# Two weight sums of the MLP's late down steps made early and kept in DRAM, and the pairs of their group in another order

## The chip, the cores and the metric

The kernel runs on one core of one Trainium2 chip. The metric is device microseconds of one execution, as the median of several runs. The engines are named as in the profile: PE is TensorE's matmul unit and PEld its weight loads, DVE is VectorE, ACT is ScalarE, POOL is GpSimd, and SP is SyncE, which here only issues DMAs.

## The reference, cut to what matters

One layer of a transformer-like trunk: a gated linear attention mixer, then a squared-ReLU MLP, each behind an RMSNorm and with a residual, and a last RMSNorm. All in float32, 256 tokens (T), model width 2048 (D), hidden width 8192.

```python
h = h + _gla_mixer(_rmsnorm(h, gla_norm[j]), ...)
h = h + _sq_relu_mlp(_rmsnorm(h, mlp_norm[i]), mlp_w_up[i], mlp_w_down[i])
return _rmsnorm(h, final_norm)

def _sq_relu_mlp(h, w_up, w_down):
    a = jax.nn.relu(h @ w_up)
    return (a * a) @ w_down
```

The change is in the last product, `(a * a) @ w_down`, of which one hidden slice and one group of 512 output columns are concerned.

## The kernel before

**Numbers.** Every float32 operand is split into two fp32r parts, `hi` (a rounded copy, made by a cast on ACT, line 123) and `lo` (the rest, a subtraction on DVE, lines 136, 170 and 1291). A product is then three matmuls: hi x hi, hi x lo, lo x hi. A matmul here is 128 rows by 256 columns (one of the 256s is T or half of a group of 512).

**Up and down steps.** The MLP runs over 8 rounds (`ROUNDS`) of 1024 hidden values. An up step takes two 128-row tiles of `w_up` for 512 hidden values, 24 matmuls; there are 128 of them (`UPS`). A down step takes a *pair* `kp` (0 to 3) of two 128-row tiles of `w_down` for a round `m` and a group `g` of 512 output columns. The program first makes 18 up steps alone (`LEAD`), and then one up step to each down step, until the up steps end; the down steps after that are alone again (`alone`). Rounds go through the groups forwards and backwards in turn, so that round 6 (`ROUNDS - 2`) ends with group 0 and round 7 begins with it.

**Two kinds of down step.** A plain one takes 2x2 blocks of activations times 2x2 blocks of weights as 8 block products, 24 matmuls. A step *by sums* (`by_sums`) does it with 7 block products of Strassen's kind, 21 matmuls, in two parts: three products from the weights as they are (9 matmuls), and four from sums and differences of the four weight blocks (12 matmuls). The sums are made in place in the raw weight tile: one block by an accumulating DMA from POOL (line 1231) and the others by two subtractions on DVE (`weight_sums`, lines 233 and 234), and are then split into hi and lo again (lines 123 and 1291). A step by sums so costs PE three matmuls less, and ACT and DVE more. Round 6's last group had one step by sums (`kp == 1`) and three plain ones; in round 7 three pairs are by sums.

In a lone step by sums the second part is issued late (`pending`): after the next step's first products.

**Sums from DRAM.** In the mixer's output product, four pairs already get their sums from DRAM: `make_sums` loads the pair in an earlier stage where the engines have time, forms the sums (line 252 and `weight_sums`), splits them (lines 255 and 259), and writes hi and lo (512 KB each) to DRAM by two DMAs from POOL (lines 256 and 260). `make_all` hands out the jobs; `MADE_AT` has, for each stage, the places in its sequence of `pump` calls (two to an up step) at which a job's two halves run. `group` reads them back into `pre` (line 330).

**Buffers.** A weight tile goes through a ring of seven raw tiles and a ring of five hi/lo pairs (pool `wpool`). An SP load waits until DVE has made `lo` from the tile that had its place; a cast waits until PE (or a DMA that reads it) is done with the hi tile. The activations of a round are two tiles `act`, tags B (pairs 0 and 1) and C (pairs 2 and 3) in the pool `big`, two buffers each.

**Order.** A scheduler with a timeline of its own orders the instructions of each engine; each engine then takes them strictly in that order, and waits by semaphores. `last_turn` (lines 978 to 987), which runs among the first lone up steps, transposes the last quarter of h (`hh`, `hl`: ACT line 856, DVE line 857) for the last two up steps of the first half-round.

Of the kernel before, what the change touches and what calls it, by code (L numbers as in the profile page):

```python
# [37 lines left out]
KT = D // P  # L38
# [9 lines left out]
G = 1024  # L48
# [21 lines left out]
def tile_gla_mlp(ctx, tc, x, xt, cols, w_vg, w_in, w_gate, w_out, w_up, w_down, final_norm, out):  # L70
# [54 lines left out]
    def slots():  # L125
        return [wpool.tile([P, SLOT], F32R, tag=i, name=i) for i in ("hi", "lo")]
# [105 lines left out]
    def weight_sums(u):  # L232
        nc.vector.tensor_tensor(u[:, 2], u[:, 0], u[:, 2], op=ALU.subtract)  # L233
        return nc.vector.tensor_tensor(u[:, 1::2], u[:, 1::2], u[:, 2:3].to_broadcast([P, 2, T]), op=ALU.subtract)  # L234
# [29 lines left out]
    def make_all():  # L264
        pair = lambda w, c0, g: w[c0 : c0 + 2 * P, g * GT : (g + 1) * GT].rearrange("(i p) c -> p i c", p=P)
        todo = [make_sums((None, g, kp), pair(w_out, 2 * kp * P, g)) for g, kp in MADE_OUT]
        todo += [make_sums((ROUNDS - 1, g, kp), pair(w_down, (ROUNDS - 1) * MR + 2 * kp * P, g)) for g, kp in MADE_DOWN]
        for places in MADE_AT:
            now = [lambda: None] * (KT - 1)
            for at in places:  # L270
                now[at], now[at + 1] = todo.pop(0)
            yield now
# [907 lines left out]
    def settle(*ks):  # L1180

        for k in ks:
            late.pop(k, lambda: None)()

    def down(passes):
# [4 lines left out]
        ahead = pending = None  # L1190
        quick = False
        units = 0
        for n, (m, g) in enumerate(passes):
            fresh = not n or passes[n - 1][1] != g
            if fresh:
# [6 lines left out]
            first = min(kp for kp in range(KP) if by_sums(m, g, kp)) if fresh else None  # L1202

            if fresh:
                quick = first == 0
            for kp in range(KP):
                last = ends and kp == KP - 1
                alone = units + LEAD >= UPS
                by_parts = by_sums(m, g, kp)

                def products(n, these, w, banks=banks, last=last):

                    with then_mm():
                        for k, o, a, c in these:
                            bank = banks[k][1]
                            for x in a[: 2 - n]:
                                for d in range(0, c.stop - c.start, T):
                                    matmul(
                                        bank[:, o + d : o + d + T], x, w[n][:, c.start + d : c.start + d + T],
                                        bank.name not in used, last and n == 1,  # L1220
                                    )
                                    used.add(bank.name)

                raw = raw_tile()[:, : 2 * GT]
                c0 = m * MR + 2 * kp * P
                src = w_down[c0 : c0 + 2 * P, g * GT : (g + 1) * GT].rearrange("(i p) c -> p i c", p=P)
                if by_parts:
                    for i in range(2):
                        last_load[0] = nc.sync.dma_start(out=raw[:, i * GT : (i + 1) * GT], in_=src[:, i])
# [5 lines left out]
                if fresh and quick and kp < 2:  # L1235
                    pass
                elif fresh and kp == 0:
                    banks.update({k: begin(k, g) for k in (B32, BX4)})
                elif fresh and kp == first:
                    settle(P16)  # L1240
                    banks[P16] = begin(P16, g)
                elif fresh and kp > first and P57 not in banks:
# [22 lines left out]
                if fresh and kp == first and not quick and not alone:  # L1265
# [5 lines left out]
                def of_sums(u=raw, products=products, at=at, kp=kp, banks=banks, quick=fresh and quick, g=g, then=ahead_of):  # L1271


                    nonlocal ahead
                    to = slots()

                    if quick and kp < 2:
                        settle((B32, P16)[kp])
                        if kp == 0:
                            banks[P57] = begin(P57, g)  # L1280
                    if then and by_sums(*then, 0):
                        ahead = {k: begin(k, then[1]) for k in (B32, P16)}
                    for a in range(2):
                        copy_hi(*(x.rearrange("p (f s) -> p f s", f=4)[:, a::2] for x in (to[0][:, :G], u)))
                    if quick and kp == 0:
                        settle(P57)
                        banks[BX4] = begin(BX4, g)
                    elif quick and kp == 1:
                        settle(BX4)
                    with tc.issue_after(last_lo[0].ins):  # L1290
                        last_lo[0] = nc.vector.tensor_tensor(to[1][:, :G], u, to[0][:, :G].bitcast(F32), op=ALU.subtract)  # L1291
                    early = (P57, 0, at(S1), block(0)), (P16, T, at(S2), block(2))
                    late = (P57, T, at(S3), block(1)), (BX4, T, at(A22), block(3))
                    products(0, early, to)
                    yield
                    products(0, late, to)
                    products(1, (*early, *late), to)

                if by_parts:
                    if alone:  # L1300

                        pending = of_sums()
                    else:
                        rest = of_sums()
                        next(rest)
                yield
                if by_parts and not alone:
                    next(rest, None)
                units += 1
                if last:  # L1310
                    if n + 1 < len(passes):
                        m1, g1 = passes[n + 1]
                        assert by_sums(m1, g1, 0) == bool(ahead)
                    else:
                        last_banks(0)
                if fresh and kp == first + alone and not quick:
                    settle(B32, BX4)
            if ends:

# [153 lines left out]
```

## Time and profile before

| | |
|---|---|
| median of 3 runs | 1040.6 us (1040.2 to 1040.94) |
| the profiled execution's own time | 1040.84 us |
| its span in the trace | 1039.1 us |
| PE busy | 1030.4 us, 99% |
| DVE, ACT, POOL busy | 903.5, 754.1, 134.4 us |
| DMA moved | 240.04 MB, mean 231 GB/s |

1.74 us of the execution lie around the span. The MLP begins at 371.3 us in the span; its lone up steps last until about 420 us, the last up step ends at 982.5 us, and the last product starts at about 1010 us. PE's busy time is wall time during which some matmul is in flight: its matmuls are pipelined, so each shows longer (276 ns) than the pace at which they follow each other.

### The profile page before, as it was taken

To read this page: it belongs to the slowest core of one execution; us is meant where nothing else is said; L and a number is where in the kernel's file an instruction comes from. 1 tells how busy PE (TensorE), PEld (TensorE's weight loads), DVE (VectorE), ACT (ScalarE), POOL (GpSimd) and SP (SyncE) were. 2 spreads that over 40 slices of the span, in tenths; PEclk is the share of its full clock that TensorE was granted. 3 is DMA by queue.
4 is the path that set the end of the run, shared out by engine and by line. 5 is a ranking of instruction groups with operands and counts; after the bars stand their busy time and mean duration, and the time that the engine had idled before them with its cause. 6 is when DMAs were issued, how large, how long until landed. Compare 5 with 4: busy or idle time off the path is not lost.

```text
span 1039.1 us, 23376 instructions
## 1 busy us (share of the span) xinstructions
PE 1030.4 (99%) x9019; PEld 1029.5 (99%) x9019; DVE 903.5 (87%) x1254; ACT 754.1 (73%) x1130; POOL 134.4 (13%) x180
## 2 busy tenths in 40 slices
PE   9999999999999999999999999999999999999997
PEld 9999999999999999999999999999999999999997
DVE  7769768898698866989989999999999999999887
ACT  7775556677576654688779788778778778778685
POOL 0000110210100001111111111111211111111100
PEclk9999999999999999999999999999999999999999
DMA  9967866758977876678888887887887888887772
GB/s 340 334 192 217 263 187 170 210 163 300 308 245 251 250 249 193 189 216 229 228 239 227 231 238 225 236 242 221 245 232 221 244 225 229 243 231 219 231 246 84
DMA packets 128591, 240.04 MB, mean 231 GB/s; under 512 B 11440, under 2 KB 30000, under 8 KB 128352
## 3 DMA queue, kind: packets, MB, share of 16 engines
q1 hardware_dynamic: 107456, 215.32, 64.2%
q0 software_dynamic: 20304, 21.64, 12.2%
q10 hardware_dynamic: 720, 1.60, 0.4%
q8 instruction: 70, 1.15, 0.4%
q14 instruction: 41, 0.34, 0.1%
HBM read 232.22 MB, written 6.29 MB: 230 GB/s over the span
## 4 chain that ended last, share of the span: by engine, by line
PE 99%; issue 0%; ACT 0%; DVE 0%; POOLq 0%; POOL 0%; DVEq 0%
PE up L1021 34%; PE acc L1021 28%; PE acc L305 16%; PE acc L181 10%; PE acc L224 6%; PE aux L224 2%; PE aux L181 1%; PE aux L843 1%; PE aux L696 1%; PE aux L399 0%; ACT sqf L1360 0%; PE acc L595 0%; DVE hf L1432 0%; POOLq L1469 0%; POOL rf L521 0%
## 5 line engine op out<-in xcount | busy, mean ns | idle before, releaser
L123 ACT CAST hi<-raw 128x1024 fp32r<-128x1024 f32 (+4 forms) x654 | 518.2, 822 | 201.1 <-DVE raw L233 66.4
L136 DVE TENSOR_TENSOR lo<-raw,hi 128x768 fp32r<-128x768 f32 (+4 forms) x228 | 233.1, 1032 | 53.6 <-ACT hi L123 50.8
L1021 PE MATMUL acc<-hi,act 128*128 128x256 f32 x1696 | 247.7, 276 | 0.0
L1021 PE MATMUL up<-hh,hi 128*128 128x256 f32 x1024 | 238.7, 276 | 0.0
L1021 PE MATMUL up<-hl,hi 128*128 128x256 f32 x1024 | 238.7, 276 | 0.0
L1021 PEld LDWEIGHTS acc<-hi,act 128*128 128x128 f32 x1696 | 217.6, 188 | 0.0
L170 DVE TENSOR_TENSOR lo<-raw,hi 128x1024 fp32r<-128x1024 f32 x160 | 194.4, 1218 | 22.5 <-ACT hi L123 21.6
L1021 PEld LDWEIGHTS up<-hh,hi 128*128 128x128 f32 x1024 | 192.3, 188 | 0.0
L1021 PEld LDWEIGHTS up<-hl,hi 128*128 128x128 f32 x1024 | 192.3, 188 | 0.0
L1231 POOL DMA_DIRECT2D raw<-in_w_down x112 | 97.1, 867 | 518.4 <-DMA raw<-in_w_down 206.2
L1291 DVE TENSOR_TENSOR lo<-raw,hi 128x1024 fp32r<-128x1024 f32 x112 | 136.3, 1217 | 1.1 <-ACT hi L123 1.1
L1021 PE MATMUL up<-hh,lo 128*128 128x256 f32 x1024 | 137.0, 276 | 0.0
L1021 PE MATMUL acc<-lo,act 128*128 128x256 f32 x848 | 133.9, 276 | 0.0
L1021 PEld LDWEIGHTS up<-hh,lo 128*128 128x128 f32 x1024 | 125.7, 188 | 0.0
L1021 PEld LDWEIGHTS acc<-lo,act 128*128 128x128 f32 x848 | 113.4, 188 | 0.0
L234 DVE TENSOR_TENSOR raw<-raw 128x512 f32<-128x512 f32 x137 | 94.5, 689 | 3.4
L233 DVE TENSOR_TENSOR raw<-raw 128x256 f32<-128x256 f32 x137 | 57.8, 422 | 13.1 <-DMA raw<-in_w_out 10.1
L181 PE MATMUL acc<-hi,xA 128*128 128x256 f32 (+1 forms) x376 | 55.6, 280 | 0.0
L181 PEld LDWEIGHTS acc<-hi,xA 128*128 128x128 f32 x376 | 49.3, 188 | 0.3 <-ACT hi L123 0.2
L224 PE MATMUL acc<-xA,hi 128*128 128x256 f32 x288 | 49.2, 276 | 0.0
L224 PEld LDWEIGHTS acc<-xA,hi 128*128 128x128 f32 x288 | 43.3, 188 | 0.0
L1148 ACT COPY sums<-acc 128x512 f32<-128x512 f32 x46 | 26.8, 583 | 22.6 <-PE acc L1021 22.5
(226 smaller groups left out, 1442.2 us busy)
## 6 DMA issues: line engine op xcount, KB each, us to landing
raw<-in_w_up SPq DMA_DIRECT2D x128, 512.0 KB, 4.3
raw<-in_w_down SPq DMA_DIRECT2D x224, 256.0 KB, 4.3
raw<-in_w_in SPq DMA_DIRECT2D x69, 512.0 KB, 4.6
raw<-in_w_down POOLq DMA_DIRECT2D x112, 128.0 KB, 5.1
raw<-in_w_out SPq DMA_DIRECT2D x22, 512.0 KB, 7.1
raw<-in_w_down SPq DMA_DIRECT2D x16, 512.0 KB, 5.2
raw<-in_w_vg SPq DMA_DIRECT2D x14, 520.0 KB, 8.6
raw<-in_w_out SPq DMA_DIRECT2D x24, 256.0 KB, 5.9
```

Of the source, the lines that this page charges most:

```text
L123: last_hi[0] = nc.scalar.copy(to, raw)
L136: last_lo[0] = nc.vector.tensor_tensor(lo[:, s], raw[:, s], hi[:, s].bitcast(F32), op=ALU.subtract)
L170: last_lo[0] = nc.vector.tensor_tensor(to[1], dst, to[0].bitcast(F32), op=ALU.subtract)
L181: newest[0] = nc.tensor.matmul(o[:, m], x, w[:, m], start=first and c == 0, stop=last, skip_group_check=True).ins
L224: nc.tensor.matmul(o, u[:, i, s], m, start=kt == 0 and n == 0 and j % 2 == 0, stop=kt == KT - 1 and n == 2, skip_group_check=True,)
L233: nc.vector.tensor_tensor(u[:, 2], u[:, 0], u[:, 2], op=ALU.subtract)
L234: return nc.vector.tensor_tensor(u[:, 1::2], u[:, 1::2], u[:, 2:3].to_broadcast([P, 2, T]), op=ALU.subtract)
L305: newest[0] = nc.tensor.matmul(bank[:, o + d : o + d + T], x, w[:, d : d + T], start=(not filled or bank in sums_banks) and bank.name not ...
L1021: newest[0] = nc.tensor.matmul(o, x, w, start=first, stop=last, skip_group_check=True).ins
L1148: last_end[0] = nc.scalar.copy(to, src).ins
L1231: nc.gpsimd.dma_start(out=raw[:, :T], in_=src[:, 0, T:], accum_op=ALU.add)
L1291: last_lo[0] = nc.vector.tensor_tensor(to[1][:, :G], u, to[0][:, :G].bitcast(F32), op=ALU.subtract)
```

## The change

Two more pairs get their sums from DRAM: pairs 0 and 1 of round 6, group 0, the last group of that round. Before, its pairs 0 (plain) and 1 (by sums, summed on the spot) went beside the last two up steps, and pairs 2 and 3 (both plain) were the first two lone steps. Now the group takes its pairs as 2, 3, 0, 1: pairs 2 (plain) and 3 (by sums, summed on the spot) go beside the last two up steps, and pairs 0 and 1 (by sums, the sums from DRAM) are the first two lone ones. So three of its four steps are by sums now, and two of them have nothing to sum on DVE, and read 1.375 MB instead of 0.5 MB. The sums are made by two more jobs at the places 10 and 16 of the lone up steps. `pre`, the tile into which they are read back, takes a buffer of tag C.

```diff
-    MADE_DOWN = ()
-    MADE_AT = ((2,), (4,), (6, 10))
+    MADE_DOWN = ((ROUNDS - 2, 0, 0), (ROUNDS - 2, 0, 1))
+    MADE_AT = ((2,), (4,), (6, 10), (10, 16))
...
+    def pairs_of(m, g):
+        return (2, 3, 0, 1) if m == ROUNDS - 2 and g == order_of(m)[-1] else range(KP)
+
     def by_sums(m, g, kp):
...
-        return m < ROUNDS - 2 or g != order_of(m)[-1] or kp == 1
+        return m < ROUNDS - 2 or g != order_of(m)[-1] or kp in (3, 0, 1)
...
-            for kp in range(KP):
+            for pos, kp in enumerate(pairs_of(m, g)):
...
-                if by_parts:
+                ready = made.get((m, g, kp))
+                if pos == 0 and any((m, g, k) in made for k in range(KP)):
+                    rooms.extend(big.tile([P, 4 * G + 64], F32R, tag="C", name="pre")[:, : 4 * G].rearrange("p (b i c) -> b p i c", b=2, i=2))
+                if ready is not None:
+                    last_load[0] = nc.sync.dma_start(out=raw[:, T:GT], in_=src[:, 0, T:])
+                    last_load[0] = nc.sync.dma_start(out=raw[:, GT:], in_=src[:, 1])
+                    ready_in = rooms.pop(0)
+                    for i in range(2):
+                        last_load[0] = nc.sync.dma_start(out=ready_in[:, i].bitcast(F32), in_=ready[i])
+                    ready = [ready_in[:, i] for i in range(2)]
+                elif by_parts:
...
-                    with tc.issue_after(last_lo[0].ins):
-                        last_sum[0] = weight_sums(u).ins
+                    if ready is None:
+                        with tc.issue_after(last_lo[0].ins):
+                            last_sum[0] = weight_sums(u).ins
...
     n_raw[0] = 0
+    jobs.extend(next(make))
     steps = up()
```

**PE, where the up steps end.** Names: `hi_`/`lo_` are parts of weights by number, `pre` the sums from DRAM, `act` the activations, `acc` the banks. Before, the first two lone down steps are plain (16 matmuls with hi, 8 with lo each):

```order
L1021 MATMUL acc_13122<-hi_13258,act_12149 128x256 x4
L1021 MATMUL acc_13124<-hi_13258,act_12149 128x256 x4
L1021 MATMUL acc_13122<-hi_13258,act_12149 128x256 x4
L1021 MATMUL acc_13124<-hi_13258,act_12149 128x256 x4
L1021 MATMUL acc_13122<-lo_13259,act_12149 128x256 x2
L1021 MATMUL acc_13124<-lo_13259,act_12149 128x256 x2
L1021 MATMUL acc_13122<-lo_13259,act_12149 128x256 x2
L1021 MATMUL acc_13124<-lo_13259,act_12149 128x256 x2
L1021 MATMUL acc_13122<-hi_13295,act_12149 128x256 x4
```

Now there stand the first parts of both steps (6 with hi and 3 with lo each), and then the first step's 12 matmuls with `pre`; the second step's 12 with `pre` come after the plain step that follows (hi_13340):

```order
L1025 MATMUL acc_13216<-hi_13286,act_11604 128x256 x2
L1025 MATMUL acc_13147<-hi_13286,act_11604 128x256 x4
L1025 MATMUL acc_13216<-lo_13287,act_11604 128x256
L1025 MATMUL acc_13147<-lo_13287,act_11604 128x256 x2
L1025 MATMUL acc_13216<-hi_13311,act_11604 128x256 x2
L1025 MATMUL acc_13147<-hi_13311,act_11604 128x256 x4
L1025 MATMUL acc_13216<-lo_13312,act_11604 128x256
L1025 MATMUL acc_13147<-lo_13312,act_11604 128x256 x2
L1025 MATMUL acc_13252<-pre_13141,act_11604 128x256 x2
```

What moved: the second lone step's weights (hi_13295 before, hi_13311 now) are asked for after 9 matmuls instead of 24. On ACT and DVE the rows stand in the same order there; the two steps' casts and subtractions are 128x768 instead of 128x1024.

**DVE, among the first lone up steps.** `lo_` from `w_up`, `hl` of the last transposed quarter of h; before:

```order
L170 TENSOR_TENSOR lo_5100<-raw_5101,hi_5099 128x1024
L976 TENSOR_SCALAR work_4913<-ident_96,r2_4912 128x128
L170 TENSOR_TENSOR lo_5130<-raw_5131,hi_5129 128x1024
L170 TENSOR_TENSOR lo_5160<-raw_5161,hi_5159 128x1024
L170 TENSOR_TENSOR lo_5193<-raw_5194,hi_5192 128x2x512
L857 SCALAR_TENSOR_TENSOR hl_4046<-aux_5064,colt_81,hh_4045 128x256
L857 SCALAR_TENSOR_TENSOR hl_4046<-aux_5065,colt_81,hh_4045 128x256
L857 SCALAR_TENSOR_TENSOR hl_4046<-aux_5064,colt_81,hh_4045 128x256
```

Now, with the semaphores that each waits for (DMASW6 is counted up by the landing of `made_1282<-lo_5121`, which POOL issues):

```order
L252 TENSOR_TENSOR raw_5115<-raw_5115 128x256 [waits DMAHW1_49]
L976 TENSOR_SCALAR work_4915<-ident_96,r2_4914 128x128 [waits Pool_49]
L233 TENSOR_TENSOR raw_5115<-raw_5115 128x256 [waits DVE_49]
L234 TENSOR_TENSOR raw_5115<-raw_5115 128x2x256 [waits DVE_49]
L259 TENSOR_TENSOR lo_5121<-raw_5115,hi_5120 128x1024 [waits PE_49,Activation_49]
L170 TENSOR_TENSOR lo_5143<-raw_5144,hi_5142 128x1024 [waits DMAHW2_49,PE_49,Activation_49]
L170 TENSOR_TENSOR lo_5173<-raw_5174,hi_5172 128x1024 [waits DMAHW3_49,PE_49,Activation_49]
L857 SCALAR_TENSOR_TENSOR hl_4048<-aux_5066,colt_81,hh_4047 128x256 [waits Activation_49]
L857 SCALAR_TENSOR_TENSOR hl_4048<-aux_5067,colt_81,hh_4047 128x256 [waits Activation_49]
L170 TENSOR_TENSOR lo_5206<-raw_5207,hi_5205 128x2x512 [waits DMAHW4_49,DMASW6_49,DVE_49]
L252 TENSOR_TENSOR raw_5227<-raw_5227 128x256 [waits DMAHW5_49]
L857 SCALAR_TENSOR_TENSOR hl_4048<-aux_5066,colt_81,hh_4047 128x256 [waits Activation_49]
```

What moved: a job's four operations stand ahead, and the third `hl` (aux_5066 the second time) stands behind a `lo` whose buffer the job's second write to DRAM must first have left, and behind the second job's first addition.

**SP, some 60 us before the group.** Loads of weights for the coming steps, and now the four loads of `pre`:

```order
L1244 DMA raw_12501<-in_w_down 128x512 [waits DMAHW1_49]
L1240 DMA pre_13141<-made_1282 128x1024 [waits DMAHW2_49,PE_49]
L1240 DMA pre_13141<-made_1282 128x1024 [waits DMAHW3_49]
L1240 DMA pre_13141<-made_1283 128x1024 [waits DMAHW4_49]
L163 DMA raw_12522<-in_w_up 128x2x512 [waits DMAHW5_49,DVE_49]
L1240 DMA pre_13141<-made_1283 128x1024 [waits DMAHW6_49]
L1244 DMA raw_12571<-in_w_down 128x512 [waits DMAHW7_49,DMASW1_49,DVE_49]
```

What moved: the first of the four waits for PE (the round-5 activations whose buffer `pre` takes), and the two weight loads behind it (raw_12498 and raw_12547 before) stand behind it on SP.

More of the change, by code (lines that the diff above doesn't have):

```diff
@@ L266, in make_all @@
         todo = [make_sums((None, g, kp), pair(w_out, 2 * kp * P, g)) for g, kp in MADE_OUT]
-        todo += [make_sums((ROUNDS - 1, g, kp), pair(w_down, (ROUNDS - 1) * MR + 2 * kp * P, g)) for g, kp in MADE_DOWN]
+        todo += [make_sums((m, g, kp), pair(w_down, m * MR + 2 * kp * P, g)) for m, g, kp in MADE_DOWN]
         for places in MADE_AT:
-            now = [lambda: None] * (KT - 1)
+            now = [lambda: None] * max(KT - 1, places[-1] + 2)
             for at in places:
@@ L1201, in down @@
             ends = n + 1 == len(passes) or passes[n + 1][1] != g
-            first = min(kp for kp in range(KP) if by_sums(m, g, kp)) if fresh else None
+            first = [by_sums(m, g, kp) for kp in pairs_of(m, g)].index(True) if fresh else None
             if fresh:
                 quick = first == 0
-            for kp in range(KP):
-                last = ends and kp == KP - 1
+            for pos, kp in enumerate(pairs_of(m, g)):
+                last = ends and pos == KP - 1
                 alone = units + LEAD >= UPS
@@ L1264, in down @@
                 yield
-                if fresh and kp == first and not quick and not alone:
+                if fresh and pos == first and not quick and not alone:
                     settle(P57)
@@ L1269, in down, with of_sums @@
                 ahead_of = passes[n + 1] if last and n + 1 < len(passes) else None
-                def of_sums(u=raw, products=products, at=at, kp=kp, banks=banks, quick=fresh and quick, g=g, then=ahead_of):
+                def of_sums(u=raw, products=products, at=at, pos=pos, banks=banks, quick=fresh and quick, g=g, then=ahead_of, to=ready):
                     nonlocal ahead
[L1275 to L1279, printed above, removed]
+                    copied = not to
+                    to = to or slots()
+                    if quick and pos < 2:
+                        settle((B32, P16)[pos])
+                        if pos == 0:
                             banks[P57] = begin(P57, g)
-                    if then and by_sums(*then, 0):
+                    if then and by_sums(*then, pairs_of(*then)[0]):
                         ahead = {k: begin(k, then[1]) for k in (B32, P16)}
-                    for a in range(2):
+                    for a in range(2 * copied):
                         copy_hi(*(x.rearrange("p (f s) -> p f s", f=4)[:, a::2] for x in (to[0][:, :G], u)))
-                    if quick and kp == 0:
+                    if quick and pos == 0:
                         settle(P57)
                         banks[BX4] = begin(BX4, g)
-                    elif quick and kp == 1:
+                    elif quick and pos == 1:
                         settle(BX4)
-                    with tc.issue_after(last_lo[0].ins):
-                        last_lo[0] = nc.vector.tensor_tensor(to[1][:, :G], u, to[0][:, :G].bitcast(F32), op=ALU.subtract)
+                    if copied:
+                        with tc.issue_after(last_lo[0].ins):
+                            last_lo[0] = nc.vector.tensor_tensor(to[1][:, :G], u, to[0][:, :G].bitcast(F32), op=ALU.subtract)
                     early = (P57, 0, at(S1), block(0)), (P16, T, at(S2), block(2))
@@ L1312, in down @@
                         m1, g1 = passes[n + 1]
-                        assert by_sums(m1, g1, 0) == bool(ahead)
+                        assert by_sums(m1, g1, pairs_of(m1, g1)[0]) == bool(ahead)
                     else:
                         last_banks(0)
-                if fresh and kp == first + alone and not quick:
+                if fresh and pos == first + alone and not quick:
                     settle(B32, BX4)
```

9 lines of the change are left out of this document (5 added, 4 removed).

## The prediction

> **What bounds the kernel now.** The page was read first: its busy shares and its chain of waits. Then the windows of four stretches, and then the timelines of PE, DVE, ACT and SP at the three places that the change touches.
>
> ```profile
> span 1039.1 us, 23376 instructions
> PE 1030.4 (99%) x9019; PEld 1029.5 (99%) x9019; DVE 903.5 (87%) x1254; ACT 754.1 (73%) x1130; POOL 134.4 (13%) x180
> PE 99%; issue 0%; ACT 0%; DVE 0%; POOLq 0%; POOL 0%; DVEq 0%
> ```
>
> PE is busy for 99% of the span, and the chain that ended last runs through PE alone. So PE's time is its number of matmuls times their pace, plus whatever it is made to wait. In the windows, each engine's busy time stands behind the length of the stretch; the last three columns are PE's granted clock, the DMA share and GB/s.
>
> ```profile
> 260.00:280.00 20.00, 20.00 (x179) 20.00 (x178) 10.74 (x12) 9.05 (x9) 2.83 (x4) 1.00 0.97 348
> 380.00:390.00 10.00, 10.00 (x91) 10.00 (x90) 5.88 (x8) 5.17 (x8) 0.00 (x0) 1.00 0.57 173
> 430.00:530.00 100.00, 100.00 (x884) 100.00 (x884) 91.22 (x117) 75.88 (x113) 16.06 (x19) 1.00 0.79 225
> 910.00:960.00 50.00, 50.00 (x444) 50.00 (x443) 47.78 (x62) 40.38 (x61) 7.80 (x9) 1.00 0.81 227
> ```
>
> From 430 to 530 us the pace is 100.00 us / 884 = 113.1 ns, at a full clock. DVE is the next engine: 91% busy there and 96% from 910 to 960 (47.78 of 50), but 59% in the lone up steps at 380 to 390, where the new jobs stand.
>
> **The matmuls removed.** Two of the group's plain steps become steps by sums, 21 matmuls instead of 24. That is 2 x 3 x 113.1 ns = 0.68 us, all on PE and so all on the path, if PE goes on without a wait. Nothing else can come off PE's time, so this is also the most that the change can gain.
>
> **The first two lone steps.** PE's side of the place, by start and duration:
>
> ```profile
> 983.39 1.98 PE L1021 MATMUL acc<-hi,act 128*128 128x256 f32 x16
> 986.11 1.98 PE L1021 MATMUL acc<-hi,act 128*128 128x256 f32 x16
> 988.83 1.41 PE L1021 MATMUL acc<-hi,act 128*128 128x256 f32 x11
> ```
>
> And what makes the parts, on DVE and on ACT, and the two rows for their shorter forms (the mean ns of one stands behind the bar):
>
> ```profile
> 979.05 1.23 DVE L136 TENSOR_TENSOR lo<-raw,hi 128x1024 fp32r<-128x1024 f32 x1 [0.55 <-ACT hi L123]
> 982.45 1.29 DVE L1111 SCALAR_TENSOR_TENSOR work<-up,work 128x512 f32<-128x512 f32 x2 [2.17 <-PE up L1021]
> 984.84 1.22 DVE L136 TENSOR_TENSOR lo<-raw,hi 128x1024 fp32r<-128x1024 f32 x1
> 987.23 1.22 DVE L136 TENSOR_TENSOR lo<-raw,hi 128x1024 fp32r<-128x1024 f32 x1
> ```
>
> ```profile
> 983.18 0.63 ACT L1122 ACTIVATE work<-work 128x512 f32<-128x512 f32 x1 [4.16 <-DVE work L1111]
> 983.72 1.03 ACT L123 CAST hi<-raw 128x1024 fp32r<-128x1024 f32 x1
> 985.01 1.05 ACT L1133 CAST act<-work 128x1024 fp32r<-128x1024 f32 x1 [0.26 <-DVE work L1126]
> 985.96 1.05 ACT L123 CAST hi<-raw 128x1024 fp32r<-128x1024 f32 x1
> ```
>
> ```profile
> L136 DVE TENSOR_TENSOR lo<-raw,hi 128x768 fp32r<-128x768 f32 x8 | 7.6, 951 | 0.2 <-ACT hi L123 0.2
> L123 ACT CAST hi<-raw 128x768 fp32r<-128x768 f32 x7 | 5.7, 831 | 0.0
> ```
>
> The first lone step's `lo` is made at 979, 4 us early. The second one's cast (983.72) stands on ACT behind a square, which had waited 4.16 us for DVE's work on the last up product; its `lo` (984.84) stands behind the same work on DVE, which had waited 2.17 us for PE. The end of the up product sets these times, and the order of both engines is unchanged there, so a shorter lone step brings neither forward. Before, PE asked for this hi at 986.11. Now it asks for it after 9 matmuls:
>
> - PE starts the first lone step at 983.39 as before (the two steps ahead have 24 + 21 matmuls in either order). 9 x 0.113 gives 984.41.
> - The second step's hi is ready at 983.72 + 0.83 = 984.55: PE waits 0.14 us. Six matmuls later it is 985.23.
> - Its lo is ready at 984.84 + 0.95 = 985.79: PE waits 0.56 us. Three matmuls end at 986.13.
> - 12 with `pre` end at 987.49. The plain step's hi is there at 985.96 + 1.05 = 987.01, and its lo at 987.23 + 1.22 = 988.45, 0.8 us ahead of its use at 989.30. With 24 + 12 more matmuls it is 991.56.
>
> Before, the same point was 988.83 + 24 x 0.113 = 991.54. The new wait of 0.70 us so takes the whole 0.68 us, and the net is +0.02 us. Its bounds: -0.68 if ACT and DVE run these two operations earlier than the walk has them, and +0.3 if the shorter forms take as long as the two rows they replace (1.03 and 1.22 us: waits of 0.34 and 0.63). I take the walk.
>
> Behind it everything stands as before. The act tile that now takes the just-freed buffer is written at 985.01, 1.5 us after PE has left it at about 983.5. `pre` is read 60 us after its loads. The smaller casts and subtractions and the missing accumulating DMA take work off ACT, DVE and POOL that PE doesn't wait for. All this is costed at nothing; if the buffer did come late, its own cast would slip, and the two casts and PE's plain steps behind it.
>
> **The two jobs among the lone up steps.** The two write rows are the landing times of hi and of lo:
>
> ```profile
> 376.27 0.28 DVE L976 TENSOR_SCALAR work<-ident,r 128x128 f32<-128x128 f32 x1
> L857 DVE SCALAR_TENSOR_TENSOR hl<-aux,colt,hh x4: 477/484/485, 384.8 to 387.9; 128x256 fp32r<-128x256 f32 x4
> 389.28 0.28 PE L1021 MATMUL up<-hl,hi 128*128 128x256 f32 x1
> 390.19 0.28 PE L1021 MATMUL up<-hl,hi 128*128 128x256 f32 x1
> ```
>
> ```profile
> L234 DVE TENSOR_TENSOR raw<-raw 128x512 f32<-128x512 f32 x8 | 5.5, 692 | 0.3
> L233 DVE TENSOR_TENSOR raw<-raw 128x256 f32<-128x256 f32 x8 | 3.4, 422 | 0.2
> ```
>
> ```profile
> DMA to landing us min/median/max: 3.1/3.8/7.0
> ```
>
> ```profile
> L260 POOL DMA_DIRECT2D made<-lo x4: 533/541/553, 95.8 to 266.3; - x4
> who waited for it (us, times):
>   DVE lo L170: 0.5, 1
> DMA to landing us min/median/max: 6.5/6.9/7.1
> ```
>
> A job costs DVE two additions, a double subtraction and a split, 0.42 + 0.42 + 0.69 + 1.22 = 2.75 us and ACT one cast; for two jobs that is 5.5 us of DVE, while in the lone steps it is free 4.1 us in every 10. PE's cost is nothing, unless the order makes something late, and one thing is near: the third `hl`, wanted at 390.19. It stands behind a `lo` whose buffer the job's second write must have left. The first job's sums follow the work at 376.27 and end at about 377.9; cast and subtraction bring it to about 380.2; POOL's issue follows some 0.3 us later, at 380.5. With landings of 6.5 to 7.1 us that is 387.0 to 387.6. Then come that `lo` (1.22), the second job's first addition (0.42) and the `hl` (0.48): 389.1 to 389.7. The margin is 0.5 to 1.1 us. The write of hi holds up a cast on ACT in the same way, with the first `hl` behind it: at 3.8 us nothing is late, at 7.0 us the cast starts at about 386.2 and the third `hl` ends some 0.4 us late. So the price is 0 to 0.4 us by the rows, and I take 0; a write that lands later costs PE one for one. The Trainium skill ("DMA: Bandwidth & Descriptors", section "Anatomy of one DMA — SWDGE (gpsimd) path") fits such a DMA with 2.0 us plus its bytes over 436,000 per us, an estimate of 3.2 us for 512 KB; by that the margin would be over 4 us and this price surely none. The four lo writes took 6.5 to 7.1 us here, twice that, and the rows decide.
>
> **The loads of `pre` on SP.**
>
> ```profile
> 907.54 4.06 SPq L163 DMA_DIRECT2D raw<-in_w_up  x2
> 912.36 0.84 SPq L1229 DMA_DIRECT2D raw<-in_w_down  x2
> ```
>
> ```profile
> 928.91 0.42 DVE L233 TENSOR_TENSOR raw<-raw 128x256 f32<-128x256 f32 x1
> 931.12 1.22 DVE L1291 TENSOR_TENSOR lo<-raw,hi 128x1024 fp32r<-128x1024 f32 x1
> 936.61 0.62 PE L1021 MATMUL acc<-lo,act 128*128 128x256 f32 x4
> 972.77 1.41 PE L1021 MATMUL acc<-hi,act 128*128 128x256 f32 x11
> ```
>
> ```profile
> raw<-in_w_down SPq DMA_DIRECT2D x224, 256.0 KB, 4.3
> raw<-in_w_down POOLq DMA_DIRECT2D x112, 128.0 KB, 5.1
> ```
>
> The first load waits until PE has done with round 5, twelve steps before 972.77: 12 x 45 x 0.113 = 61.1 us earlier, at 911.7. SP gets there at about 908 and stands for some 4 us. The w_up load behind it and the two w_down loads of 912.36 slip by about 1.2 us of issue, and 2 MB of `pre` go ahead of them, 6 us at the 348 GB/s of the busiest window: up to 7.2 us. The sum of that pair starts on DVE at 928.91, though its data were there at about 912.4 + 4.3 + 5.1 + 1 = 922.8: a lead of 6.1 us. So DVE slips by at most 1.1 us, and the `lo` that follows ends at 932.34 before, 4.3 us ahead of PE's use at 936.61. Price 0; without that last cover it would be 1.1 us.
>
> **The sum.** -0.68 + 0.70 + 0 + 0 = +0.02 us on the profiled execution's 1040.84 us, or 1040.9. That execution lies 0.24 us above the median of 1040.6; against the median the forecast is 1040.6, and I give 1040.7, since the terms taken at nothing can add and not gain.
>
> **The rivals.**
>
> *The gain comes through.* ACT or DVE would have to pass the second lone step's two operations ahead of the up product's work, or PE to arrive later for another reason. The order speaks against it; that 0.14 + 0.56 us is a small wait, read from one execution, speaks for it. 1040.6 - 0.7 = 1039.9.
>
> *The first job's writes land late, and PE stalls at 390 us* (slower). For it: both writes share a queue with loads, hi writes spread from 3.1 to 7.0 us, and in before a DVE operation already waited 0.5 us for such a landing. Against it: the slowest landings belong to a stage with 348 GB/s, and here there are 173. Beyond a landing of about 8 us, every microsecond is one of PE's. A landing worse than the slowest by as much as the spread (7.1 + 3.9 = 11 us) would cost 2.8 to 3.4 us. It ends between 1040.8 and 1044, with 1041.8 as the likeliest; a loss over 2.08 us needs a landing of about 9.7 us.
>
> *The backlog reaches PE.* The two jobs, or the 2 MB of `pre`, use up leads while DVE is at 91 to 96% and can't regain them: 910 to 960 leaves it 2.2 us free in 50. Against it: 4.3 us of lead at the place. 1.1 us more than forecast, 1041.7; twice that if two of these fall together.
>
> **How the numbers follow.** The likeliest case, the gain eaten by the new wait, has 0.50 (own range 1040.3 to 1041.1); the gain coming through 0.13; the late write 0.27, of which 0.10 costs over 2.08 us; the backlog 0.10, of which 0.05. 0.2% of the time, 2.08 us, is about what a measurement of this kernel can tell from no change. No case gains that much (0.01 is left for it), 0.15 lose it, and 0.84 lie within. The range is 1039.8 (the gain whole) to 1042.8 (the late write up to its bound), and leaves out the dearest part of two rivals.
>
> **What would show it.** Right: near 984 to 986 PE has about 0.7 us of waits for ACT's cast and DVE's subtraction of the second lone step, and reaches the next round at the time of before. No such wait, and a span of 1038.4, is the first rival. PE waiting near 389 to 391 for `hl` is the second, with the landing of the two `made` writes of 379 to 381 us as its size. SP standing at the `pre` load until about 912 is expected; a PE wait for `lo` between 925 and 945 is the third rival. The prediction is wrong in its base if PE's matmuls change their pace, or if PE waits anywhere else.

## The result, and the profile after

The changed kernel took 1044.27 us (median of 7 runs, 1042.85 to 1044.69) against 1040.6 (median of 7, 1040.17 to 1041.28): a ratio of 1.0031, with a 95% interval of 1.0022 to 1.004. The forecast was 1040.7, from 1039.8 to 1042.8. Measured again on two other occasions the ratio was 1.0014 (1.0005 to 1.0023) and 1.0025 (1.0009 to 1.004). So it is slower, by some 2.0 us for a reason that belongs to the change, and in the profiles of the first comparison by another 1.4 us that does not.

The page of after: the span, the busy times, the chain.

```profile
span 1042.4 us, 23391 instructions
PE 1033.4 (99%) x9013; PEld 1032.4 (99%) x9013; DVE 907.9 (87%) x1262; ACT 755.7 (72%) x1132; POOL 136.7 (13%) x184
PE 98%; issue 0%; DMA 0%; DVE 0%; ACT 0%; SPq 0%; POOLq 0%; POOL 0%; DVEq 0%
```

PE has six matmuls fewer and is busy 3.0 us longer. The table of PE's waits (us in total, times, longest) has one row more than before, and it is short:

```profile
PE acc L1025 <- DVE lo L136: 0.3, 1, 0.3
```

So little of the time went into waits. Two windows show where it went: 205 to 245 us, in the mixer, and 990 to 1025 us, behind the lone steps. First before, with a third window that is looked at below, then after:

```profile
205.00:245.00 40.00, 40.00 (x355) 40.00 (x354) 35.85 (x52) 27.46 (x41) 5.50 (x6) 1.00 0.71 220
303.00:312.00 9.00, 9.00 (x79) 9.00 (x78) 8.19 (x13) 6.03 (x10) 0.86 (x1) 1.00 1.00 297
990.00:1025.00 35.00, 35.00 (x312) 35.00 (x311) 30.75 (x40) 26.86 (x44) 0.88 (x1) 1.00 0.54 169
```

```profile
205.00:245.00 40.00, 40.00 (x342) 40.00 (x341) 34.66 (x49) 26.65 (x40) 4.92 (x7) 1.00 0.68 212
990.00:1025.00 35.00, 35.00 (x300) 35.00 (x299) 29.93 (x39) 27.02 (x43) 0.86 (x1) 1.00 0.54 171
```

PE is busy for the whole of each window and its granted clock is 1.00, but after has 342 matmuls where before has 355, and 300 where before has 312. (A window also counts the two or three matmuls that are in flight at its start.) The starts of single matmuls lie 113.3 ns apart in the one and 117.8 in the other, 3.8% of the time. From 350 to 985 us, by contrast, the starts of the two kernels' matmuls keep a constant distance of 1.42 us; at the last matmul it is 3.39 us. PE has two paces, and "busy" does not tell them apart.

The slow pace at the end begins exactly where the prediction had its new wait. PE, ACT and DVE of after:

```profile
984.80 0.84 PE L1025 MATMUL acc<-hi,act 128*128 128x256 f32 x6
985.48 0.50 PE L1025 MATMUL acc<-lo,act 128*128 128x256 f32 x3
986.00 0.97 PE L1025 MATMUL acc<-hi,act 128*128 128x256 f32 x6
987.26 0.62 PE L1025 MATMUL acc<-lo,act 128*128 128x256 f32 x3 [0.28 <-DVE lo L136]
987.73 1.57 PE L1025 MATMUL acc<-pre,act 128*128 128x256 f32 x12
989.14 0.63 PE L1025 MATMUL acc<-hi,act 128*128 128x256 f32 x4
```

```profile
985.13 0.82 ACT L123 CAST hi<-raw 128x768 fp32r<-128x768 f32 x1
```

```profile
986.25 0.95 DVE L136 TENSOR_TENSOR lo<-raw,hi 128x768 fp32r<-128x768 f32 x1
```

The first lone step begins at 984.80 (983.39 before; everything here is 1.42 us later). The second one's hi starts at 986.00 instead of 985.82, since its cast ends at 985.95: 0.18 us. Its lo starts at 987.26 instead of 986.82: 0.44 us. Behind each wait the second matmul follows after some 225 ns instead of 113, another 0.11 us each time. That is 0.84 us of waits. The twelve on `pre` then take 1.41 us from 987.73 to 989.14, 117.5 ns each, and so it goes on to the last matmul at 1034.6: 46.9 us x 3.8% = 1.8 us. The sum at the end: -0.68 + 0.84 + 1.8 = +2.0 us, as the distance says (3.39 - 1.42 = 1.97).

The other 1.4 us arise at 203 us, some 160 us ahead of the first instruction that the change moves. What comes late there is a POOL instruction; before, then after:

```profile
196.63 0.86 POOL L335 DMA_DIRECT2D raw<-in_w_in  x1 [5.82 <-DMA raw<-in_w_in]
197.54 0.93 POOL L521 TENSOR_TENSOR ors<-oss,mhalf 128x1 f32<-128x1 f32 x1
```

```profile
197.61 0.86 POOL L335 DMA_DIRECT2D raw<-in_w_in  x1 [6.09 <-DVE oss L792]
198.17 1.54 POOL L521 TENSOR_TENSOR ors<-oss,mhalf 128x1 f32<-128x1 f32 x1
```

A weight load landed 0.9 us later in this execution (5.3 and 5.5 us after its issue for the two halves, 4.4 and 4.6 before; the row names DVE's `oss`, which ended about then), POOL issued its accumulating DMA later, and the norm's `ors` stood behind it. PE then waited 0.14 us for the product of that norm at 202.9, and its pace was 117.8 ns from there to 248 us: 2.0 us in all, of which 0.6 come back between 297 and 315 us, where before has short waits of PE, most of which after has not. The experiments show that the late stretch comes and goes from execution to execution, in the kernel before too.

### The profile page after: what moved, and what is told of

Read it like the earlier page. It is cut to its first block, busy times and chain, and to the rows that moved or that the text cites. A ratio compares the mean times of both kernels' runs of the same rounds, so it can differ in the third digit from the quotient of the medians.

```text
span 1042.4 us, 23391 instructions
## 1 busy us (share of the span) xinstructions
PE 1033.4 (99%) x9013; PEld 1032.4 (99%) x9013; DVE 907.9 (87%) x1262; ACT 755.7 (72%) x1132; POOL 136.7 (13%) x184
## 4 chain that ended last, share of the span: by engine, by line
PE 98%; issue 0%; DMA 0%; DVE 0%; ACT 0%; SPq 0%; POOLq 0%; POOL 0%; DVEq 0%
PE up L1025 33%; PE acc L1025 27%; PE acc L305 16%; PE acc L181 10%; PE acc L224 6%; PE aux L224 2%; PE aux L181 1%; PE aux L843 1%; PE aux L696 1%; DMA raw<-in_w_vg 0%; ACT sqf L1379 0%; SPq L173 0%; DVE lo L136 0%; PE acc L595 0%; SPq L460 0%
```

## The experiments

Theory 1: a short wait of PE can leave it at the slower pace for a long time, so a wait costs far more than itself. Theory 2: a wait costs itself, and the slow stretches are something else. All comparisons are with runs of the kernel before on the same chip at the same time.

**A wait put into the middle of the MLP.** The kernel before, with one weight cast repeated.

```diff
+                n_pairs[0] += 1
+                for _ in range(7 if n_pairs[0] == STALL else 1):
+                    copy_hi(to[0], dst)
-                copy_hi(to[0], dst)
```

> The kernel before, with one weight cast of an up step repeated seven times on ACT (the same output), so that PE must wait once, some 2 to 4 us, at about 642 us of the span. Theory 1 (a wait of PE in the stretch of 128x256 matmuls leaves it at a slower pace, 117.8 instead of 113.3 ns a matmul, until one of the short 120 ns episodes that the trace of before shows at 607 and 975 us): the pace stays at 117.8 from the wait to about 975 us, and the run takes the wait plus 333 us x 3.9% = 13 us, about 1055 to 1058 us. Theory 2 (the slow stretches of the changed kernel are a drift of the chip, and a wait costs only itself): 1043 to 1045 us, with 113.3 ns on both sides of the wait.

Measured: 1059.07 us (1057.96 to 1062.53, 4 runs), ratio 1.0171 (1.0155 to 1.0186). Its windows in the mixer, at the wait and behind it, then before's window behind that place, and the wait:

```profile
205.00:245.00 40.00, 40.00 (x342) 40.00 (x341) 34.74 (x50) 26.66 (x40) 4.99 (x7) 1.00 0.69 212
647.00:650.40 3.40, 3.40 (x16) 3.40 (x17) 2.54 (x3) 3.40 (x6) 0.00 (x0) 0.50 0.31 93
650.00:950.00 300.00, 300.00 (x2548) 300.00 (x2547) 275.12 (x356) 230.29 (x338) 49.40 (x57) 1.00 0.80 225
```

```profile
650.00:950.00 300.00, 300.00 (x2650) 300.00 (x2649) 284.27 (x370) 238.07 (x350) 51.14 (x59) 1.00 0.83 233
```

```profile
PE up L1024 <- ACT hi L123: 3.0, 1, 3.0
```

The kernel before has 2650 matmuls in that window of 300 us; here there are 2548, at a clock of 1.00. A wait of 3 us cost 18 us. Two things stand beside each other: the granted clock fell to 0.50 for 3.4 us, and was 1.00 again from 650.4 us on; the pace of 117.8 ns stayed, and not only to 975 us, as I had expected, but to the end. So theory 2 doesn't hold here. The first row is a by-product: the mixer of this kernel is that of before, and it has the slow stretch at 203 us in this execution. Since the clock was lowered too, a shorter wait was tried.

**The same with five casts, and with a group of short matmuls behind it.** Both cast five times instead of seven; the second run also splits eight matmuls into sixteen, by these lines.

```diff
+                    cut = P if n_pairs[0] == STALL + 5 and i == n == 0 else T
+                    for d in range(0, T, cut):
...
+                            o[:, d : d + cut], w[n][:, i, j * P : (j + 1) * P], a[:, 2 * kp + i, d : d + cut],
```

> The run with one weight cast repeated, with five casts instead of seven (the same output), so that PE's one wait at about 642 us is some 0.5 to 1 us and too short to lower the granted clock. If a wait of any length leaves PE at the slower pace: 117.8 ns from there to the end, 390 us x 3.9% = 15 us, about 1056 us in all. If it was the 3 us of wait and the lowered clock that did it in the first of these runs: 1041 to 1042 us, at 113.3 ns.

> The run with five casts, and five up steps behind the repeated cast eight 128x256 matmuls are made as sixteen of 128x128 (the same products; about 0.8 us of PE). In the trace of before, groups of 128x128 matmuls stand where the slow stretches end (248 and 313 us). If such a group ends the slow pace: 117.8 ns from 642 to about 668 us only, 113.3 ns behind it, and about 1043 us in all, some 13 us less than without the split. If the slow pace ends for another reason: 1057 us.

Measured: five casts, 8 runs: seven from 1041.11 to 1044.02 us and one of 1058.82. With the split, 2 runs: 1054.87 and 1055.91. The window behind the wait, first of the five casts and then of the split:

```profile
650.00:950.00 300.00, 300.00 (x2650) 300.00 (x2649) 285.62 (x371) 239.69 (x353) 51.74 (x60) 1.00 0.84 235
```

```profile
650.00:950.00 300.00, 300.00 (x2550) 300.00 (x2549) 274.00 (x355) 230.86 (x338) 48.67 (x56) 1.00 0.81 226
```

Both have the same wait of 0.9 us, at a granted clock of 1.00, and with the split the pace is 117.8 ns from the wait on, ahead of the split. So neither expectation was right as it stood: behind the same wait one profile goes on fast and the other slow, and then some 15 us are lost. By their times seven of the eight runs with five casts went on fast; the eighth, 1058.82, has no profile, but its time is about what the slow pace would make. The short matmuls at 670 us ended nothing. In that run the slow pace ended at 993 us, the place of a short run of 120 ns matmuls that stands at 975 to 978 us in before (15 us earlier); in the run with seven casts it went on behind the same place. What such a run is isn't known.

**The waits at the end taken away.** The changed kernel, with the second part of a lone step from DRAM made at once; PE then asks for the second lone step 1.4 us later.

```diff
+                    if alone and ready is not None:
+                        for _ in of_sums():
+                            pass
-                    if alone:
+                    elif alone:
```

> The changed kernel, but a lone step whose sums come from DRAM makes its second part at once instead of behind the next step's first part: PE has 21 matmuls (2.38 us) between its first and its second demand and so asks for the second lone step's parts at about 985.8 and 986.4 instead of 984.4 and 985.2. Theory 1: no wait of PE there, the pace stays at 113.3 ns to the end, and the gain of 0.68 us remains at this place: 1.87 us less than the changed kernel (its profiled end lost 0.70 us of waits and about 1.8 us of pace, and won 0.68), so 1042.4 if the slow stretch of 203 to 252 us stays, and 1039.9 to 1040.4 if that too is gone. Theory 2 (only the waits count): 0.7 us less than the changed kernel, 1043.5.

> The changed kernel once more, for a second profile. Theory 1 at the end: again 0.6 to 0.8 us of waits at about 985 and 117.8 ns from there to the end. If the stretch of 203 to 252 us belongs to the kernel, it is there again; if to the run, it may be gone, and the span is then 1.4 us shorter.

> The changed kernel with the second parts at once, a second time, beside the changed kernel on the same chip. No wait at the end, 113.3 ns there: 0.7 us of waits and 1.8 us of pace less than the changed kernel, and 0.68 us less than before (six matmuls), in executions of one kind at 203 to 252 us.

> The changed kernel a third time: waits of 0.7 us at 986 and 117.8 ns behind them; 1.9 us more than before in executions of one kind at 203 to 252 us.

Measured: at once 1040.22 and 1039.87 us (11 runs each), the changed kernel beside it 1042.73 and 1042.53 (10 and 12 runs), before 1041.39 and 1040.59. PE at once, and its window at the end:

```profile
985.88 1.52 PE L1025 MATMUL acc<-pre,act 128*128 128x256 f32 x12
987.24 0.84 PE L1025 MATMUL acc<-hi,act 128*128 128x256 f32 x6
987.92 0.50 PE L1025 MATMUL acc<-lo,act 128*128 128x256 f32 x3
```

```profile
990.00:1025.00 35.00, 35.00 (x312) 35.00 (x311) 31.37 (x42) 27.77 (x45) 0.86 (x1) 1.00 0.55 173
```

No wait, 312 matmuls, and 2.5 and 2.7 us less than the changed kernel: 0.84 of waits and 1.8 of pace. (My 1.87 in the first expectation had the gain of 0.68 taken off once too often.) This is the change's whole loss, and without it the 0.68 us come through: 0.9990 of before (0.9981 to 0.9998) in the second comparison, 0.9993 (0.9984 to 1.0001, which takes in no change) in the first. The traces are sharper: from 978 us to the last matmul the distance to the matmuls of before shrinks by 0.68 us in both profiles at once, and grows by 1.96 to 1.97 us in all three of the changed kernel.

One of the changed kernel's runs in the second comparison, 1051.23 us, lies far above the others and has no profile; what happened in it isn't known. The two further profiles of the changed kernel have 300 matmuls in the window at the end, like the first, but 356 and 355 from 205 to 245 us. Here is the first of them:

```profile
205.00:245.00 40.00, 40.00 (x356) 40.00 (x355) 35.76 (x52) 27.29 (x40) 6.41 (x6) 1.00 0.70 215
990.00:1025.00 35.00, 35.00 (x300) 35.00 (x299) 30.01 (x39) 26.14 (x43) 0.00 (x0) 1.00 0.51 163
```

So the slow end belongs to the kernel, and the slow stretch at 203 us to the execution. The times say it too: the 27 runs of before that stood beside the first four experiments lie at 1040.0 to 1041.0 (13 of them) and at 1041.4 to 1042.9 (14). The first at once and the two with seven and five casts, whose mixers are unchanged, have 342 matmuls there in their profiles. Why the first comparison had the slow stretch in nearly all seven runs of after, by their times, and in none of before, isn't shown.

**The jobs alone.** The jobs run, and nothing reads their results; the group is as before.

```diff
-        return (2, 3, 0, 1) if m == ROUNDS - 2 and g == order_of(m)[-1] else range(KP)
+        return range(KP)
...
-                ready = made.get((m, g, kp))
+                ready = None
```

> The changed kernel's two jobs among the lone up steps (loads, sums, casts, four writes of 512 KB to DRAM), whose results are not read: the group keeps the pairs and steps of before. If the jobs or the places of the two new DRAM tiles cause the slow stretch of 203 to 252 us (its order of instructions is the same in both kernels): about 1042 us, with that stretch at 117.8 ns. If that stretch comes and goes by itself from run to run: 1040.6 us in most runs. If the jobs make something late at about 390 us, a wait of PE stands there, and the pace behind it is 117.8 until an episode ends it.

Measured: 1040.41 us against 1041.39, ratio 0.9994 (0.9985 to 1.0003), no wait of PE in the MLP, 355 matmuls from 205 to 245 us. The jobs cost nothing that can be seen.

**One wait at the end of the kernel before.** The second lone step's cast is made three times.

```diff
+            for _ in range(times):
+                copy_hi(hi[:, s], raw[:, s])
...
+                w = parts(..., 3 if (m, g, kp) == (ROUNDS - 2, 0, 3) else 1)
```

> The kernel before, with the cast of the second lone step's weights made three times (the same output), so that PE waits once, some 0.5 us, at 986 us; nothing else is changed. If one wait there is enough for the slower pace to the end: 0.5 + 1.8 = 2.3 us more than before in most executions, and 117.8 ns from 986 us on in the profile. If a wait leaves the pace as it was in most executions, as in the run with five casts at 642 us: 0.5 us more in most of them, and two groups of times.

```profile
986.28 2.15 PE L1022 MATMUL acc<-hi,act 128*128 128x256 f32 x16 [0.69 <-ACT hi L123]
```

```profile
990.00:1025.00 35.00, 35.00 (x299) 35.00 (x298) 31.13 (x41) 27.61 (x45) 0.88 (x1) 1.00 0.56 176
```

Measured: 1041.71 us, 11 runs: eight from 1041.44 to 1041.78 and three from 1042.83 to 1044.69. The profiled one, 1042.83, has 299 matmuls behind the wait. The wait is 0.97 us with the slower second matmul; from before's lower group (some 1040.3) that gives 1041.3 at the fast pace and 1043.1 at the slow, so by their times the eight went on fast, and the profiled one did not. The wait alone, in a kernel that has nothing else of the change, is enough for the slow pace, but not in every execution.

**One of the two waits taken from the changed kernel, and a second one put into the kernel before.**

```diff
                         pending = of_sums()
+                        if ready is not None:
+                            next(pending)
```

> The changed kernel with four of the first lone step's twelve matmuls on pre ahead of the second lone step's first part, so that PE asks for that step's hi 0.45 us later and doesn't wait for it, and waits only for its lo, some 0.3 us. If two waits in a row are what makes the slower pace sure: two groups of times as after one wait, most of them some 2 us below the changed kernel. If this kind of wait (for the moving operand, in the middle of a step) makes it sure by itself: all times 0.4 to 0.5 us below the changed kernel, at 117.8 ns behind it.

> The kernel before with the wait of 0.97 us for the second lone step's hi (cast made three times), and its subtraction made twice, so that PE waits again for lo, some 0.2 to 0.5 us (the same output). If a second wait makes the slower pace sure: all times at least 1.0 + 0.3 + 1.7 = 3.0 us above before, and the profile at 117.8 ns from the second wait on. If each wait only has its own chance: two groups again, the lower one some 1.3 us above before, with fewer executions in it than after one wait.

Measured: with the wait for lo alone (0.42 us) 1041.79 us, 12 runs from 1041.32 to 1043.61, against 1040.69, ratio 1.0007 (0.9998 to 1.0016). In the profile:

```profile
986.17 0.84 PE L1025 MATMUL acc<-hi,act 128*128 128x256 f32 x6
987.15 0.62 PE L1025 MATMUL acc<-lo,act 128*128 128x256 f32 x3
```

```profile
990.00:1025.00 35.00, 35.00 (x300) 35.00 (x299) 30.38 (x39) 26.93 (x44) 0.86 (x1) 1.00 0.55 172
```

The lower group of before lay at some 1040.4 beside it. At the fast pace that of this run would be at 1040.4 - 0.68 + 0.42 = 1040.1, and none is there; at the slow pace at 1041.9, about where it is. So, by these times, a single wait for lo was followed by the slow pace in all runs or nearly all, and two in a row aren't needed. With two waits in the kernel before: 1044.02 us, 10 runs from 1042.71 to 1045.8; PE also waited a third time, further on, so the groups can't be read. Its profile ran at 117.8 ns from the first wait on. This one is inconclusive. What makes the slow pace sure after one wait (for lo, in a step by sums) and rare after another (for hi, in a plain step) stays open.

**Short matmuls to end the slow pace.** Four matmuls behind the changed kernel's wait split in two, and six in the first product of the run at once.

```diff
+                            cut = P if cutting and n == 0 and a is these[0][2] else T
...
+                                fine[0] = ahead is not None and step == 5 and t == 0 and i < 2 and c not in odd
```

> The changed kernel with four matmuls of the first plain step of round 7 (at about 988 us, behind the wait) made as eight of 128x128 (the same products; 0.4 us of PE). If the short ones end the slow pace: 113.3 ns from about 990 us on, 1.8 - 0.4 - 0.1 = 1.3 us less than the changed kernel, about 1041.2 us. If eight are too few or it isn't they that end it: 0.4 us more than the changed kernel.

> The run without the wait at the end (second parts at once), and in the first product six matmuls of the sixth step (at about 20 us, in the slow stretch from 5 to 63 us) made as twelve of 128x128 (the same products; 0.6 us of PE). If the short ones end the slow pace there: 42 us x 3.8% - 0.6 = 1.0 us less than without them, 1039.2 us. If the matmuls of 272 columns in every step of that product bring the slow pace back: 0.6 us more, 1040.8 us.

Measured: 1043.01 us (ratio 1.0026, 1.0016 to 1.0036) and 1042.99 us (1.0021, 1.0012 to 1.003). Neither ended it. At the end the pace stayed at 117.8. In the first product it was no better, and worse behind it: from 70 to 140 us there are 597 matmuls where before has 619, so the slow pace that ends at 63 us in before went on to 150 us.

```profile
70.00:140.00 70.00, 70.00 (x597) 70.00 (x596) 52.38 (x89) 39.71 (x44) 5.58 (x21) 1.00 0.76 231
```

**The jobs moved behind the last transposes.** At once, and `MADE_AT`'s last entry (19, 27) instead of (10, 16).

> The changed kernel with the second parts at once, and the two jobs at the places 19 and 27 of the lone up steps instead of 10 and 16, so that no hl stands behind a job's write. If the jobs cost PE nothing at the one place or the other: the time of the run without the move. If the late write costs now and then (a wait of 0.2 us and 7.5 us at the slower pace in one profile): the same median within 0.3 us, and never a wait for hl at 390 us in the profile. If the later jobs reach into the stage behind (their last write lands some 10 us later): a wait of PE between 410 and 440 us.

Measured: 1040.18 us beside 1039.87 without the move, ratio to before 0.9992 (0.9984 to 1.0001), no wait of PE in the MLP. It makes no difference that can be measured.

## Why the prediction was wrong, step by step

**What failed: the pace behind the wait.** The sum put the new wait against the removed matmuls and multiplied everything else by 113.1 ns: "Behind it everything stands as before." The waits were where the walk had them, and the 47 us behind them were not as before: 117.8 ns a matmul instead of 113.3, at the same granted clock. That one step cost 1.8 us of the 2.0 that belong to the change. The prediction named it as what would make it wrong in its base, and gave it no price and no chance. Yet the trace of before had the second pace in it. The window from 303 to 312 us, shown above, has 79 matmuls in 9 us at a granted clock of 1.00; at 113.3 ns there would be 82 (9 us / 113.3 ns, and two or three in flight). And it stands behind two short waits, in before's PE:

```profile
301.05 0.28 PE L305 MATMUL acc<-hi,otl 128*128 128x256 f32 x1
301.21 0.74 PE L305 MATMUL acc<-lo,oth 128*128 128x256 f32 x4
302.02 0.40 PE L305 MATMUL acc<-hi,otl 128*128 128x256 f32 x2
302.34 0.50 PE L305 MATMUL acc<-lo,oth 128*128 128x256 f32 x2
```

The starts at 301.21 and 302.34 are 0.04 and 0.09 us late, which the table of waits doesn't list; the matmul behind each follows after some 225 ns, and the others up to 312.7 us after 117.8 ns. I took PE's pace from one window of 100 us and read "busy 99%" as "at its pace" in the others.

**Mis-sized: the wait.** 0.84 us instead of 0.70. The casts and subtractions started within 0.02 us of the walk (985.13 and 986.25, less 1.42); what it lacked is the second matmul behind each wait, 0.11 us late.

**Right: the removed matmuls.** 0.68 us, which the run at once shows in full. **Right: no gain, with the reason that was given.** The second lone step is asked for after 9 matmuls, and neither ACT nor DVE has it ready.

**Right: the loads of `pre`.** SP and DVE of after:

```profile
913.18 1.27 SPq L1240 DMA_DIRECT2D pre<-made  x3
```

```profile
931.70 0.42 DVE L233 TENSOR_TENSOR raw<-raw 128x256 f32<-128x256 f32 x1 [1.60 <-DMA raw<-in_w_down]
```

SP stood until 911.76 on before's scale (911.7 forecast), and the block sum came 1.37 us late (at most 1.1 forecast) after a wait for the load behind `pre`. PE did not wait.

**Right in kind, not the cause: the late write.** The first job's lo write landed 6.3 to 7.3 us after its issue in eight of the nine profiles with the jobs at those places, and 7.8 us in one, the run with the split at the end. There DVE and PE have what the rival said:

```profile
PE up L1025 <- DVE hl L857: 0.2, 1, 0.2
```

The threshold of about 8 us, less a few tenths of hand-overs, held. The price was 0.45 us at PE (0.34 of wait, and the second matmul 0.11 late) and some 7 us at the slow pace, which ended at 398 us. In the profile with 7.3 us, the second at once, PE did not wait, but its pace turned slow at 390.4 us, just where it comes to this `hl`.

**Not seen at all: the stretch at 203 us.** The instructions there are the same, so the forecast took their time as fixed. A landing 0.9 us later made the whole 1.4 us longer, and this moves the first comparison from +2.0 to +3.4 us in the profiles (+3.7 in the medians). The three runs of before, one of them profiled and at the fast pace there, and the others at times like its own, did not show it.

## What to carry to other kernels

Where PE is the bound, count its matmuls per window beside its busy share and its granted clock, in every stage: two windows with the same kind of matmuls should have the same count. Price a short wait of PE by what may follow it, up to the next place where the pace was seen to recover, and not by its length: with one wait of 0.42 us left, the change that removes six matmuls was no faster than before. An order that gives a late operand one more step of other work in front (here the 12 matmuls on `pre` that were ready) was worth 2.5 us here, and not only the 0.84 us of waits.

## What the runs showed of the hardware that was not expected

A matmul of 128 x 256 in fp32r follows the last after 113.3 ns or after 117.8 ns, at the same granted clock of 1.00, for tens to hundreds of us. In the fast pace the next weight load starts 3 to 4 ns behind a matmul's start, in the slow one 2 to 3 ns. A wait as short as 0.04 us (before, at 301.2 us) was followed by the slow one; a wait of 0.9 us often wasn't. And a wait isn't always there: in the second profile at once the starts from 390.2 us on go from 113 to 115, 116, 117 and 118 ns apart, with no gap between them, and the pace stays at 117.8 ns until 396.5 us. Why there are two paces, and what picks one, isn't shown.

The Trainium skill ("TensorE: Matmul & The Clock Gate", section "HAM oscillation — how this bites in real kernels") has the rule that PE should have no idle gaps above some 3.4 us. The granted clock here agrees roughly: a wait of 3.0 us, somewhat less than that, lowered it for 3.4 us, and those of 0.97 us and less didn't. For the time the rule isn't enough here: waits of 0.14 to 0.97 us were followed by 3.8% less pace with the clock at 1.00, and the measurement decides.
